# One trunk layer on one core: values of a head and output gates of its neighbour in one unit of 512 streamed columns

## The chip, the cores and the metric

The kernel runs on one core of one Trainium2 chip. The metric is the device time of one execution in microseconds (us); lower is better. All matrix products run in fp32r, each as three products of high and low parts (high x high, high x low, low x high), so that the result has nearly fp32's precision.

## The reference

One layer (DEPTH = 1): an mLSTM token mixer with a residual norm, then a top-2 mixture of 16 experts, then a gated embedding. The change lies in the mixer's input projection. Cut to that:

```python
# x: (1, 1024, 1024); A_HEADS = 4, A_DK = 128, A_DV = 256
def mlstm_mixer(x, w_in, conv_w, gate_b, norm_g, w_out):
    z = x @ w_in
    qk, v, o, gates = jnp.split(z, [2 * nqk, 2 * nqk + nv, 2 * nqk + 2 * nv], axis=-1)
    qk = silu(causal_depthwise_conv(qk, conv_w))
    ...
    h = mlstm_chunkwise(q, k, v, log_i, log_f)      # needs q, k, v of the head, and the gates
    y = head_rms_norm(h, norm_g) * sigmoid(o)       # o: output gates, 256 columns for each head
    return y @ w_out
```

## The kernel before

The 1024 tokens are eight tiles (t) of 128; the model width is eight blocks (k) of 128. `x` lies transposed in SBUF as high and low parts (XH, XL). The mixer works by units, each a slice of the input projection's columns:

- `qk_units` (u = 0 to 7: query and key of a head): the weights are the stationary operand, 512 tokens stream past them.
- `v_unit(h)` (256 columns of values; head 0 has the 8 gate columns besides): for each tile 24 products (eight k, three terms), with a block of x as the stationary operand and 256 columns of weights streaming. The result goes to VH, VL.
- `o_unit(h)` (256 columns of output gates): the same 24 products for each tile; ScalarE takes the sigmoid (`sg`), SyncE writes it to DRAM (`sig_d`).

`load_w` brings a raw piece of at most 1056 columns by SyncE's queue (`wr`, 3 buffers), ScalarE makes its high part (`wh`, 4 buffers), VectorE its low part (`wl`, 4 buffers). A unit of 256 columns has two pieces of four k each; a query or key unit has one.

`rec(h)` is the recurrence of a head over eight chunks: score, numerator (`nu`) and state update (`U`) on TensorE with small steps on ScalarE, VectorE and GpSimd between them; each chunk's numerator is written to DRAM (`num_d`). The code's order is

```python
        for h in range(H):
            rec(h)
            if h + 1 < H:
                v_unit(h + 1)
            if h + 2 < H:
                qk_units(2 * h + 4)
                qk_units(2 * h + 5)
            else:
                o_unit(h - 2, o_weights(h - 2))
        w2 = o_weights(2)
        pr.close()
```

so gates of heads 0 and 1 are traced within the loop, those of heads 2 and 3 behind it. The kernel is built with a list scheduler: it sets each engine's instruction order when the kernel is built, and mixes a recurrence with the unit that follows it; on the chip each engine runs its order as it stands.

`pr.close()` gives back the recurrence's memory. The output projection's weights take its room (`wout` pool; `load_wout`, L426): eight pieces through the same three `wr` buffers, ScalarE makes `woh` (scaled by the norm's gain `ng`), VectorE makes `wol`. `hs` (in the tile `spc`) is the heads' norm factor, from the denominators and sums of squares of all chunks of all heads. `mixed(t)` loads a tile's numerators (`nm`) and gates (`sgm`), multiplies them with `hs`, and splits them into `yh` (ScalarE) and `yl` (GpSimd for tile 0, VectorE for tile 1); TensorE transposes them (`tr`), ScalarE evicts (`yt`). `project` is the output projection of a tile: 24 products of 512 columns for each half of the model width, in the order of k, which read `woh` and `wol` of that k.

Of the kernel before, what the change touches and what calls it, by code (L numbers as in the profile page):

```python
# [13 lines left out]
F32 = mybir.dt.float32  # L14
# [10 lines left out]
D = 1024  # L25
NT = T // 128
ND = D // 128
H = 4
# [17 lines left out]
def trunk(ctx, tc, io, out):  # L46
# [77 lines left out]
    # ------------------------------------------------ token mixer  # L124
    pw = ExitStack()
    with ExitStack() as pa:
# [34 lines left out]
        def first_load():  # L161
            """the first units' weights and columns of x, in the order of their use"""
# [18 lines left out]
        def qk_units(*us, first=False, between=lambda: None):  # L181
            """the convolved queries or keys of heads; between is traced after half of the products"""
# [28 lines left out]
        def vo_weights(src, n):  # L211
            w = [load_w(src[:, 4 * i:4 * i + 4], 4 * n) for i in range(2)]
            return [[t.rearrange("p (k c) -> p k c", k=4) for t in p] for p in w]

        def vo_product(ps, w, t):
            half, o = divmod(t, 4)
            for k in range(ND):
                wh, wl = w[k // 4]
                xh = XH[half][:, k, 128 * o:128 * o + 128]
                xl = XL[half][:, k, 128 * o:128 * o + 128]  # L220
                product(ps, [(xh, wh[:, k % 4]), (xh, wl[:, k % 4]), (xl, wh[:, k % 4])],
                        k == 0, k == ND - 1)
# [3 lines left out]

        def v_unit(h):
            n = 264 if h == 0 else 256
            w = vo_weights(io["wv0"] if h == 0 else io["wv"][h - 1], n)
            for t in range(NT):  # L230
                ps = pmm.tile([128, 512], F32, name="mm")
                vo_product(ps[:, :n], w, t)
                vh = rp.tile([128, 258], F32R, name="vh", bufs=9)
# [8 lines left out]
        def o_weights(h):  # L242
            return vo_weights(io["wo"][h], 256)

        def o_unit(h, w):
            for t in range(NT):
                ps = pmm.tile([128, 512], F32, name="mm")
                vo_product(ps[:, :256], w, t)
                sg = wpool.tile([128, 256], F32, name="sg", bufs=2)
                S.activation(sg, ps[:, :256], AF.Sigmoid)  # L250
                SP.dma_start(sig_d[t, :, h], sg)
# [6 lines left out]
        def gates():  # L258
            """the gates' running sums and maxima, in two steps"""
# [125 lines left out]
        for h in range(H):  # L385
# [8 lines left out]
            if h + 2 < H:  # L394
                qk_units(2 * h + 4)
                qk_units(2 * h + 5)
            else:
                o_unit(h - 2, o_weights(h - 2))
        w2 = o_weights(2)
        pr.close()  # L400

        # output projection's weights and first rows, beside the last of the input projection
# [33 lines left out]
        o_unit(2, w2)  # L436
        for k in range(ND):
            if k == 2:
                w3 = o_weights(3)
            load_wout(k)  # L440

        def turned(src, q, hi, lo, n=128):
            """the parts of the transposes of four blocks of columns"""
# [5 lines left out]
        def transposed(p, hi, lo, tagbase):  # L449
            """the transposes of [128, D] parts, and the steps that make them"""  # L450
# [14 lines left out]
        def mixed(t, p):  # L465
            """a tile's gated heads and their parts, in steps; the last leaves the transposes"""
# [13 lines left out]
        o_unit(3, w3)  # L480
# [12 lines left out]
    # ------------------------------------------------ experts' parts  # L493
# [10 lines left out]
    def new_piece(kind):  # L504
        """kind: 0 and 1 for the first products' weights, 2 for the second's"""
# [7 lines left out]
    def queue_piece(raw, shape, kind, eng=None):  # L513
        """a piece whose split is queued, to be traced among the products"""
# [16 lines left out]
    def use(piece):  # L531
        """a piece's parts, after its split"""
# [4 lines left out]
    def splits(n):  # L537
        """the next n of the queued splits"""
# [3 lines left out]
    def tick():  # L542
        """after a step of products: every second a queued split, if the clock runs"""
# [6 lines left out]
    def load_part(fetch, m, eng=None, kind=None):  # L550
        """the two pieces of an expert's m-th weights"""
# [9 lines left out]
    def find_tokens(e, parts, nt=NT, p=None, pi=None):  # L561
        """tokens of slots: e [128 tokens, nt, slots] marks a slot's token; parts: ranges of slots"""
# [1152 lines left out]
```

## Time and profile before

| | |
|---|---|
| time, median of 3 runs | 1011.89 us (1011.25 to 1013.51) |
| span of the profiled execution | 1008.3 us |
| its own time: span and what lies around it | about 1011.9 us (3.6 us around the span, from the median) |
| TensorE busy | 973.3 us (97%), 5596 matmuls |
| VectorE, ScalarE, GpSimd busy | 667.0, 561.8, 302.0 us |
| mixer, up to the first transposes of the gated heads | 0 to 330.4 us |

A matmul's busy time overlaps its neighbours', so TensorE's pace is read from the distance of two starts and not from the mean duration. An instruction waits for the one ahead of it on its engine, also where that one waits for another engine or a DMA.

### The profile page before, as it was taken

What the parts mean: (1) busy time and instruction counts of PE and PEld (TensorE: products, weight loads), DVE (VectorE), ACT (ScalarE), POOL (GpSimd) and SP (SyncE); (2) the same over time, 40 slices, a digit from 0 to 9 for tenths busy, and PEclk for the clock granted to TensorE, in tenths of its full rate; (3) what the DMA queues carried; (4) which work ended last, traced back from release to release, by engine and by line L of the source; (5) the groups of instructions that cost most, each with busy time, mean ns of one, the idle gap of its engine ahead of it and who ended that gap; (6) DMA issues with size and microseconds to landing.
All of it is one profiled execution on the core that took longest, in us unless ns stands there. A gap on an engine that the chain in (4) does not pass through costs nothing. (4 is left out here: it accounts for less than half of the span.)

```text
span 1008.3 us, 15211 instructions
## 1 busy us (share of the span) xinstructions
PE 973.3 (97%) x5596; PEld 823.0 (82%) x5596; DVE 667.0 (66%) x1217; ACT 561.8 (56%) x928; POOL 302.0 (30%) x269
## 2 busy tenths in 40 slices
PE   7999999999999999997789999999999999989998
PEld 5989999899999887886467687878787878767887
DVE  6567667461542578879966689866657575577883
ACT  6346546363562455665447666766767676653431
POOL 0002203030100112225647424334252524354442
PEclk9999999999999999999979999999999999999999
DMA  8126811203354364522657998989898988754531
GB/s 320 47 69 266 305 58 59 84 33 93 101 183 155 136 251 150 187 67 117 223 177 289 377 330 290 342 290 335 297 336 298 342 325 296 268 194 149 184 127 63
DMA packets 51396, 207.05 MB, mean 205 GB/s; under 512 B 6892, under 2 KB 15724, under 8 KB 38264
## 3 DMA queue, kind: packets, MB, share of 16 engines
q1 hardware_dynamic: 43720, 182.74, 50.4%
q0 software_dynamic: 5824, 21.50, 6.1%
q10 hardware_dynamic: 1776, 1.81, 0.5%
q8 instruction: 45, 0.74, 0.3%
q14 instruction: 31, 0.25, 0.1%
HBM read 170.35 MB, written 35.68 MB: 204 GB/s over the span
## 5 line engine op out<-in xcount | busy, mean ns | idle before, releaser
L523 POOL TENSOR_TENSOR wlo<-wraw,whi 128x1024 fp32r<-128x1024 f32 x64 | 166.2, 2615 | 223.9 <-ACT whi L522 211.4
L522 ACT ACTIVATE whi<-wraw 128x1024 fp32r<-128x1024 f32 x204 | 205.5, 1051 | 12.9 <-DMA wraw<-eu 4.3
L523 DVE TENSOR_TENSOR wlo<-wraw,whi 128x1024 fp32r<-128x1024 f32 x140 | 172.5, 1259 | 38.8 <-ACT whi L522 37.7
L63 PE MATMUL mm<-whi,xt 128*128 128x512 f32 (+1 forms) x528 | 171.9, 396 | 2.2 <-DVE xt L58 1.5
L63 PE MATMUL mm<-wl,xh 128*128 128x256 f32 (+1 forms) x512 | 145.9, 285 | 0.0
L63 PE MATMUL mm<-wh,xh 128*128 128x256 f32 (+1 forms) x512 | 145.6, 284 | 0.0
L63 PE MATMUL mm<-wh,xl 128*128 128x256 f32 (+1 forms) x512 | 145.4, 284 | 0.0
L63 PEld LDWEIGHTS mm<-whi,xt 128*128 128x128 f32 x528 | 98.6, 191 | 23.7 <-DVE xt L58 2.0
L63 PE MATMUL mm<-wlo,xt 128*128 128x512 f32 (+1 forms) x264 | 100.9, 391 | 4.5 <-DVE wlo L523 4.5
L63 PEld LDWEIGHTS mm<-wh,xh 128*128 128x128 f32 x512 | 97.0, 189 | 0.1
L63 PEld LDWEIGHTS mm<-wl,xh 128*128 128x128 f32 x512 | 96.9, 189 | 0.1
L63 PEld LDWEIGHTS mm<-wh,xl 128*128 128x128 f32 x512 | 96.9, 189 | 0.0
L63 PE MATMUL mm<-woh,yt 128*128 128x512 f32 x256 | 93.6, 412 | 0.0
L63 PE MATMUL mm<-whi,ht 128*128 128x512 f32 x240 | 87.4, 413 | 2.3 <-ACT ht L57 1.4
L63 PE MATMUL mm<-whi,x2t 128*128 128x512 f32 (+1 forms) x272 | 84.7, 386 | 0.4 <-ACT x2t L57 0.4
L63 PEld LDWEIGHTS mm<-wlo,xt 128*128 128x128 f32 x264 | 49.5, 191 | 14.2 <-DVE wlo L523 4.9
L63 PEld LDWEIGHTS mm<-whi,x2t 128*128 128x128 f32 x272 | 50.1, 188 | 11.2 <-ACT x2t L57 0.9
L58 DVE TENSOR_TENSOR wl<-wr,wh 128x1024 fp32r<-128x1024 f32 (+2 forms) x26 | 29.7, 1144 | 44.3 <-ACT wh L57 44.0
L63 PE MATMUL mm<-xh,wh 128*128 128x512 f32 x128 | 50.7, 405 | 7.1 <-ACT xh L57 7.1
L63 PEld LDWEIGHTS mm<-whi,ht 128*128 128x128 f32 x240 | 45.5, 190 | 13.5 <-ACT ht L57 2.0
L63 PEld LDWEIGHTS mm<-woh,yt 128*128 128x128 f32 x256 | 48.1, 188 | 8.8
L63 PE MATMUL mm<-whi,xm 128*128 128x512 f32 x128 | 52.7, 412 | 0.0
(381 smaller groups left out, 2042.2 us busy)
## 6 DMA issues: line engine op xcount, KB each, us to landing
wraw<-eg SPq DMA_DIRECT2D x32, 1024.0 KB, 7.0
wraw<-ed SPq DMA_DIRECT2D x32, 1024.0 KB, 6.3
wraw<-eu SPq DMA_DIRECT2D x31, 1024.0 KB, 6.5
y_d<-zt SPq DMA_DIRECT2D x16, 512.0 KB, 5.6
y_d<-yo SPq DMA_DIRECT2D x14, 512.0 KB, 6.2
num_d<-nb SPq DMA_DIRECT2D x32, 128.0 KB, 1.8
wr<-wo SPq DMA_DIRECT2D x8, 512.0 KB, 4.6
sig_d<-sg SPq DMA_DIRECT2D x32, 128.0 KB, 1.8
```

The source lines that it names most:

```text
L58: (eng or V).tensor_tensor(lo, src, f32(hi), op=ALU.subtract)
L63: PE.matmul(ps, a, b, start=start and i == 0, stop=stop and i == n - 1)
L522: S.activation(hi[:, c], raw[:, c], AF.Copy)
L523: e.tensor_tensor(lo[:, c], raw[:, c], f32(hi)[:, c], op=ALU.subtract)
```

## The change

The output gates no longer have units of 256 columns. Values of head 1 and gates of head 0 share a unit of 512 columns, as do values of head 2 and gates of head 1; values of head 3 stay a unit of 256; gates of heads 2 and 3 are one unit of 512 behind the loop. A piece of weights still has 1024 columns, so a unit of 512 has four pieces of two k each. The unit with both gates has its weights asked for (`w2`) after the values of head 3, and there is nothing else behind `rec(3)` in the loop. The host's layout of the weights follows. (The change also drops comments and docstrings, which moves line numbers.)

```diff
-        def vo_weights(src, n):
-            w = [load_w(src[:, 4 * i:4 * i + 4], 4 * n) for i in range(2)]
-            return [[t.rearrange("p (k c) -> p k c", k=4) for t in p] for p in w]
-
-        def vo_product(ps, w, t):
+        def vo_weights(src):
+
+            n = src.shape[2]
+            m = 1056 // n
+            w = [load_w(src[:, m * i:m * i + m], m * n) for i in range(ND // m)]
+            return m, [[t.rearrange("p (k c) -> p k c", k=m) for t in p] for p in w]
+
+        def vo_product(ps, mw, t):
             half, o = divmod(t, 4)
+            m, w = mw
             for k in range(ND):
-                wh, wl = w[k // 4]
+                wh, wl = (a[:, k % m] for a in w[k // m])
...
+        def gate_rows(t, ps, *hs):
+
+            for i, h in enumerate(hs):
+                sg = wpool.tile([128, 256], F32, name="sg", bufs=2)
+                S.activation(sg, ps[:, 256 * i:256 * i + 256], AF.Sigmoid)
+                SP.dma_start(sig_d[t, :, h], sg)
+
         def v_unit(h):
-            n = 264 if h == 0 else 256
-            w = vo_weights(io["wv0"] if h == 0 else io["wv"][h - 1], n)
+
+            src = io["wv0"] if h == 0 else io["wvo"][h - 1] if h < H - 1 else io["wv3"]
+            n = src.shape[2]
+            w = vo_weights(src)
             for t in range(NT):
                 ps = pmm.tile([128, 512], F32, name="mm")
                 vo_product(ps[:, :n], w, t)
+                if n == 512:
+                    gate_rows(t, ps[:, 256:], h - 1)
...
-        def o_unit(h, w):
+        def o_unit(w):
+
             for t in range(NT):
                 ps = pmm.tile([128, 512], F32, name="mm")
-                vo_product(ps[:, :256], w, t)
-                sg = wpool.tile([128, 256], F32, name="sg", bufs=2)
-                S.activation(sg, ps[:, :256], AF.Sigmoid)
-                SP.dma_start(sig_d[t, :, h], sg)
+                vo_product(ps, w, t)
+                gate_rows(t, ps, H - 2, H - 1)
...
                 qk_units(2 * h + 5)
-            else:
-                o_unit(h - 2, o_weights(h - 2))
-        w2 = o_weights(2)
+            elif h + 1 < H:
+                w2 = vo_weights(io["woo"])
         pr.close()
...
-        o_unit(2, w2)
+        o_unit(w2)
         for k in range(ND):
-            if k == 2:
-                w3 = o_weights(3)
             load_wout(k)
...
-        o_unit(3, w3)
         yt, chain = list(mixed(0, yp))[1]
```

TensorE, the end of `rec(3)` before: the last of its numerators stands here among the products of the unit of head 1's gates (256 columns).

```order
L63 MATMUL mm<-wl,xh_118 128x256
L63 MATMUL nu<-CL,sh 128x258
L63 MATMUL nu<-CH,sl 128x258
L63 MATMUL nu<-vh,ph 128x258
L63 MATMUL nu<-vl,ph 128x258
L63 MATMUL nu<-vh,pl 128x258
L63 MATMUL mm<-wh,xl_120 128x256
```

Behind these rows stand 399 more products of 256 columns (the rest of that unit and the units of heads 2 and 3), and then the transposes of the first gated tile:

```order
L63 MATMUL mm<-wh,xl_120 128x256
L459 MATMUL tr<-identr,yh 128x128 x4
L459 MATMUL tr<-identr,yl 128x128 x4
L459 MATMUL tr<-identr,yh 128x128 x4
L459 MATMUL tr<-identr,yl 128x128 x4
L63 MATMUL mm<-woh_3982,yt_4276 128x512
```

TensorE, the same place with the change: `rec(3)` is spread over the eight tiles of the unit of both gates, and its last numerator stands in the last of them, behind two of that tile's 24 products.

```order
L63 MATMUL mm<-wh,xh_118 128x512
L63 MATMUL mm<-wl,xh_118 128x512
L63 MATMUL nu<-CL,sh 128x258
L63 MATMUL nu<-CH,sl 128x258
L63 MATMUL nu<-vh,ph 128x258
L63 MATMUL nu<-vl,ph 128x258
L63 MATMUL nu<-vh,pl 128x258
L63 MATMUL mm<-wh,xl_120 128x512
```

The tile's other 21 products follow, and then the same transposes, with two products of the output projection among them:

```order
L63 MATMUL mm<-wh,xl_120 128x512
L466 MATMUL tr<-identr,yh 128x128 x4
L63 MATMUL mm<-woh_3618,yt_3676 128x512
L63 MATMUL mm<-wol_3619,yt_3676 128x512
L812 MATMUL pi<-cs,ones 128x32
L466 MATMUL tr<-identr,yl 128x128 x4
L466 MATMUL tr<-identr,yh 128x128 x4
L466 MATMUL tr<-identr,yl 128x128 x4
L63 MATMUL mm<-woh_3618,yt_3677 128x512
```

So between the last numerator and the first transpose stood 400 products of 256 columns, and now stand 22 of 512.

ScalarE behind the last numerator's eviction (`nb`, `sq`), before: the eight `woh` stand among the gates' sigmoids (`sg`), and `yh` of tile 0 behind all of them.

```order
L351 ACTIVATE sq,spc<-nu 128x256
L57 ACTIVATE wh<-wr 128x1024
L250 ACTIVATE sg<-mm 128x256
L409 DMA ng<-ng 128x8
L412 DMA rr<-rw 128x128
L413 DMA lncol<-lncol 128x16
L421 ACT_TABLE_LOAD
L421 ACTIVATE tmp<-tmp,epsc 128x32
L250 ACT_TABLE_LOAD
L250 ACTIVATE sg<-mm 128x256
L431 ACTIVATE woh_3982<-wr,ng 128x1024
L431 ACTIVATE woh_3988<-wr,ng 128x1024
```

With the change, behind the same eviction and the three DMA issues and the square root, two sigmoids are left; three `woh` stand ahead of them and five among the evictions of the transposes (`yt`) that the output projection reads.

```order
L440 ACTIVATE woh_3630<-wr,ng 128x1024
L234 ACT_TABLE_LOAD
L234 ACTIVATE sg<-mm 128x256 x2
L798 DMA st_3730<-st 32x16
L57 ACTIVATE yh<-nm 128x1024
L57 ACTIVATE RW<-gr 128x8x16
L440 ACTIVATE woh_3636<-wr,ng 128x1024
L467 ACTIVATE yt_3676<-tr 128x512
L440 ACTIVATE woh_3642<-wr,ng 128x1024
L467 ACTIVATE yt_3677<-tr 128x512
L467 ACTIVATE yt_3676<-tr 128x512
L467 ACTIVATE yt_3677<-tr 128x512
```

Behind these rows stand `woh` of k = 5 and 6, `yh` of tile 1, and `woh` of k = 7. VectorE's order there is `wol` 0, `nm` of tile 0, the router's weights, `wol` 1 to 4, `nm` of tile 1, `wol` 5 and 6, `yl` of tile 1, `wol` 7. SyncE's is `nm`, `sgm` of tile 0, `wr` 3, the last tile's two gate writes, `sgm` of tile 1, `wr` 4 and 5, `nm` of tile 1, `wr` 6 and 7.

## Rows read from the trace of the kernel before

**Rows 1.** The head of the profile's page: the span, and the busy time of the engines (share of the span, instructions).

```profile
span 1008.3 us, 15211 instructions
PE 973.3 (97%) x5596; PEld 823.0 (82%) x5596; DVE 667.0 (66%) x1217; ACT 561.8 (56%) x928; POOL 302.0 (30%) x269
```

**Rows 2.** Busy time by window, for the mixer from the first pass of the recurrence on (84 to 307 us) and for the last output-gate unit (307 to 331 us): window, its length, then for each engine the busy microseconds and, in brackets, the instructions; then the granted TensorE clock (1.00 is 2.4 GHz), the DMA engines' busy share and GB/s.

```profile
84.00:307.00 223.00, 223.00 (x1699) 214.99 (x1698) 120.08 (x279) 118.19 (x306) 35.23 (x103) 1.00 0.38 129
307.00:331.00 24.00, 24.00 (x207) 24.00 (x206) 7.07 (x19) 5.89 (x13) 2.40 (x1) 1.00 0.39 125
```

**Rows 3.** Timeline of TensorE (start, duration, line, operation) in the last output-gate unit: the first and the last of its 192 products of 256 columns, 191 steps apart.

```profile
307.56 0.28 PE L63 MATMUL mm<-wh,xh 128*128 128x256 f32 x1
...
330.27 0.28 PE L63 MATMUL mm<-wh,xl 128*128 128x256 f32 x1
```

**Rows 4.** Timeline of TensorE in the query and key units of heads 2: 18 products of 512 columns right behind the recurrence's own products (17 steps), and 47 further on (46 steps).

```profile
125.00 0.40 PE L63 MATMUL mm<-xl,wh 128*128 128x512 f32 x1
...
128.95 0.39 PE L63 MATMUL mm<-xh,wh 128*128 128x512 f32 x1
129.18 0.39 PE L63 MATMUL mm<-xl,wh 128*128 128x512 f32 x1
...
139.60 0.39 PE L63 MATMUL mm<-xh,wl 128*128 128x512 f32 x1
```

**Rows 5.** Timeline of TensorE where the mixer ends: the recurrence's last product of the last head, the first transpose of tile 0's gated heads, and of the output projection's first 24 products (columns 0 to 511 of tile 0) the first and the last (the first of the two in its row).

```profile
282.72 0.28 PE L63 MATMUL nu<-vh,pl 128*128 128x258 f32 x1
...
330.39 0.46 PE L459 MATMUL tr<-identr,yh 128*128 128x128 f32 x4
...
332.06 0.46 PE L63 MATMUL mm<-woh,yt 128*128 128x512 f32 x1
...
337.72 0.63 PE L63 MATMUL mm<-woh,yt 128*128 128x512 f32 x2
```

**Rows 6.** Timeline of ScalarE (ACT; ACTq is its queue of DMA issues) from the recurrence's last eviction on.

```profile
283.04 0.38 ACT L348 ACTIVATE nb<-nu 128x256 f32<-128x256 f32 x1 [1.28 <-PE nu L63]
...
283.59 0.20 ACT L351 ACTIVATION_READ_ACCUMULATOR sq<-nu 128x1 f32 x1
...
284.94 0.39 ACT L250 ACTIVATE sg<-mm 128x256 f32<-128x256 f32 x1 [0.20 <-PE mm L63]
...
286.28 1.28 ACT L421 ACT_TABLE_LOAD   x1 [0.96 <-issue]
287.58 0.32 ACT L421 ACTIVATE tmp<-tmp,epsc 128x32 f32<-128x32 f32 x1
...
289.49 2.18 ACT L431 ACTIVATE woh<-wr,ng 128x1024 fp32r<-128x1024 f32 x2
...
309.56 0.64 ACT L250 ACTIVATE sg<-mm 128x256 f32<-128x256 f32 x2
...
319.36 1.06 ACT L57 ACTIVATE yh<-nm 128x1024 fp32r<-128x1024 f32 x1 [2.60 <-DVE nm L472]
...
331.04 1.09 ACT L460 ACTIVATE yt<-tr 128x512 fp32r<-128x512 f32 x2
332.01 0.31 ACT L57 ACTIVATE RW<-gr 128x128 fp32r<-128x128 f32 x1
```

**Rows 7.** Timeline of VectorE (DVE): a low part of the output projection's weights, tile 0's gated heads (four instructions in one row), and the router's weights (two).

```profile
309.74 1.28 DVE L432 SCALAR_TENSOR_TENSOR wol<-wr,ng,woh 128x1024 fp32r<-128x1024 f32 x1 [1.50 <-ACT woh L431]
317.65 1.67 DVE L472 SCALAR_TENSOR_TENSOR nm<-nm,spc,sgm 128x256 f32<-128x256 f32 x4 [6.63 <-DMA sgm<-sig_d]
...
328.30 0.42 DVE L800 TENSOR_TENSOR gr<-rr,lncol 128x128 f32<-128x128 f32 x2
```

**Rows 8.** Timeline of GpSimd (POOL): the low part of tile 0's gated heads.

```profile
320.50 2.40 POOL L58 TENSOR_TENSOR yl<-nm,yh 128x1024 fp32r<-128x1024 f32 x1 [44.07 <-ACT yh L57]
```

**Rows 9.** DMA issues between 225 and 345 us: target<-source, queue, count, KB of one, median us from issue to landing.

```profile
nm<-num_d SPq DMA_DIRECT2D x3, 512.0 KB, 7.2
sgm<-sig_d SPq DMA_DIRECT2D x3, 512.0 KB, 3.6
...
ng<-ng ACTq DMA_DIRECT2D x1, 4.0 KB, 3.8
```

**Rows 10.** The tile `wr`, raw pieces of weights, between 225 and 345 us: its DMA issues, and the time from issue to landing.

```profile
L428 SPq DMA_DIRECT2D wr<-wout x8: 328/333/1428, 236.2 to 302.6; - x8
...
DMA to landing us min/median/max: 3.6/5.0/5.9
```

**Rows 11.** Busy time by window (columns as in rows 2) around 490 to 510 us.

```profile
490.80:494.20 3.40, 3.40 (x7) 1.99 (x7) 3.32 (x3) 1.87 (x4) 3.05 (x2) 0.50 1.00 410
501.50:506.20 4.70, 0.38 (x2) 0.00 (x0) 4.70 (x7) 0.84 (x1) 2.91 (x2) 0.81 0.31 124
506.20:510.00 3.80, 2.10 (x4) 1.40 (x5) 3.80 (x10) 2.17 (x3) 0.00 (x0) 0.50 0.29 41
```

**Rows 12.** Timeline of TensorE inside the first of those windows.

```profile
493.08 0.63 PE L63 MATMUL mm<-whi,xm 128*128 128x512 f32 x1
493.51 0.63 PE L63 MATMUL mm<-wlo,xm 128*128 128x512 f32 x1
```

**Rows 13.** What VectorE waited for between 345 and 470 us, the longest sum: us in total, times, longest.

```profile
DVE zres L843 <- PE mm L63: 8.9, 10, 2.1
```

More of the change, by code (lines that the diff above doesn't have):

```diff
@@ L209, in qk_units @@
                 QK[u] = a
-        def vo_weights(src, n):
-            w = [load_w(src[:, 4 * i:4 * i + 4], 4 * n) for i in range(2)]
-            return [[t.rearrange("p (k c) -> p k c", k=4) for t in p] for p in w]
-        def vo_product(ps, w, t):
+        def vo_weights(src):
[4 more added lines that the diff above has]
+        def vo_product(ps, mw, t):
             half, o = divmod(t, 4)
+            m, w = mw
             for k in range(ND):
-                wh, wl = w[k // 4]
+                wh, wl = (a[:, k % m] for a in w[k // m])
                 xh = XH[half][:, k, 128 * o:128 * o + 128]
                 xl = XL[half][:, k, 128 * o:128 * o + 128]
-                product(ps, [(xh, wh[:, k % 4]), (xh, wl[:, k % 4]), (xl, wh[:, k % 4])],
-                        k == 0, k == ND - 1)
+                product(ps, [(xh, wh), (xh, wl), (xl, wh)], k == 0, k == ND - 1)
         VH, VL = {}, {}
         zg = rp.tile([128, NT, 2 * H], F32, name="zg", bufs=1)
+        def gate_rows(t, ps, *hs):
[3 more added lines that the diff above has]
+                SP.dma_start(sig_d[t, :, h], sg)
         def v_unit(h):
-            n = 264 if h == 0 else 256
-            w = vo_weights(io["wv0"] if h == 0 else io["wv"][h - 1], n)
+            src = io["wv0"] if h == 0 else io["wvo"][h - 1] if h < H - 1 else io["wv3"]
+            n = src.shape[2]
+            w = vo_weights(src)
             for t in range(NT):
@@ L240, in v_unit @@
                 VH[h, t], VL[h, t] = vh, vl
-        def o_weights(h):
-            return vo_weights(io["wo"][h], 256)
-        def o_unit(h, w):
+        def o_unit(w):
             for t in range(NT):
                 ps = pmm.tile([128, 512], F32, name="mm")
-                vo_product(ps[:, :256], w, t)
-                sg = wpool.tile([128, 256], F32, name="sg", bufs=2)
-                S.activation(sg, ps[:, :256], AF.Sigmoid)
-                SP.dma_start(sig_d[t, :, h], sg)
+                vo_product(ps, w, t)
+                gate_rows(t, ps, H - 2, H - 1)
         g4 = lambda name: rp.tile([128, NT, H], F32, name=name, bufs=1)
@@ L1671, in _layout @@
     d["wv0"] = kp(np.concatenate([w[:, v0:v0 + DV], w[:, g0:]], axis=1))
-    d["wv"] = np.stack([kp(w[:, v0 + h * DV:v0 + h * DV + DV]) for h in range(1, H)])
-    d["wo"] = np.stack([kp(w[:, o0 + h * DV:o0 + h * DV + DV]) for h in range(H)])
+    wv, wo = ([w[:, c + h * DV:c + h * DV + DV] for h in range(H)] for c in (v0, o0))
+    d["wvo"] = np.stack([kp(np.concatenate([wv[h], wo[h - 1]], axis=1)) for h in range(1, H - 1)])
+    d["wv3"] = kp(wv[H - 1])
+    d["woo"] = kp(np.concatenate(wo[H - 2:], axis=1))
     cv = c(mlstm_conv)[0].T.reshape(2, H, 128, 4)
```

## Prediction

> **What bounds the kernel now.** I read the page's head first: TensorE is busy 97% of 1008.3 us [rows 1]. A busy share says little about pace, so the windows come next. From 84 to 331 us TensorE has no idle time at all, while VectorE works 120 of 223 us in the first stretch and only 7.1 of 24 in the second, ScalarE 118 and 5.9 [rows 2]. The mixer is bound by how fast TensorE takes its columns, and its last 24 us leave the other engines nearly free. The timeline then gives the pace. 256 columns: 191 steps from 307.56 to 330.27 us, 118.9 ns each [rows 3]. 512 columns: 17 steps beside the recurrence in 3.95 us, 232.4 ns, and 46 quiet steps in 10.42 us, 226.5 ns [rows 4]. Both run at the full clock. Last I read the end of the mixer on each engine [rows 5 to 8], since the change moves what stands there.
>
> **What the streams gain.** Before, seven units (three of values, four of gates) have 8 x 24 products of 256 columns, 1344 in all. Now three units have 192 of 512 columns and one has 192 of 256. So 1152 products of 256 become 576 of 512. A pair of the old took 2 x 118.9 = 237.8 ns [rows 3]. The trace has no 512-column product with these operands; the nearest rows bound it between 226.5 and 232.4 ns [rows 4]. In all three units a recurrence runs beside for most of the time, so I weight the row beside it twice: 230.5 ns. The gain is 576 x 7.3 ns = 4.2 us, between 3.1 (232.4) and 6.5 (226.5). The Trainium skill, "TensorE: Matmul & The Clock Gate", section "Back-to-back issue gap", gives columns over 2.4 GHz and 2.5 ns for a product alone: 109.2 and 215.8 ns. The rows are 8 to 9% above at 256 columns and 5 to 8% at 512; by the page a pair would save 2.5 ns, and the gain would be an estimated 1.5 us instead of 4.2.
>
> **What costs nothing.** Pieces of weights stay fourteen, each with the same split; sigmoids stay 32 of 256 columns, now two waits on a tile fewer. A unit of 512 takes all four `wh` and `wl` buffers, so the next unit's pieces are split only while its last tile runs. The first piece is free with 18 products left, 4.1 us; a split takes 1.06 us on ScalarE and 1.23 on VectorE (the second piece's shape, [rows 6, 7], is the same 1024 columns at 1.1 and 1.3 us). That is hidden. Without the cover each unit's start would cost some 2.4 us, four times. The recurrence's small steps have more time than before: a chunk falls on a tile of 24 x 230.5 ns = 5.5 us.
>
> **The hole behind the mixer.** Before, rec(3) issues its last numerator at 282.72 us and the first transpose of tile 0 comes at 330.39 [rows 5]: 47.7 us of gate products, in which ScalarE and VectorE prepare the eight pieces of output weights, `hs`, and tile 0. With the change 22 products of 512 stand there, 5.1 us. The preparation reads chunk 8's sums and takes the recurrence's memory, so in the new order it still starts behind the last numerator. I count from the issue of that numerator and take each step from the rows:
> - ScalarE's evictions end at 1.1 (283.79 - 282.72) [rows 6]. The gain `ng` is asked for then and lands 3.8 us later [rows 9]: 4.9. Three DMA issues, the table load of 1.28 us and the root fit ahead of that.
> - `woh` 0 to 2 at 1.09 us [rows 6]: 8.2. Table load for the sigmoid 1.28, two sigmoids 0.64, a DMA issue 0.4: 10.5. `yh` 1.06: 11.6. RW 0.3: 11.9 [rows 6].
> - VectorE meanwhile: `wol` 0 until 7.3 (1.28), `nm` 1.67 until 9.0, router 0.42, `wol` 1 until 10.6, `wol` 2 until 11.8 [rows 7].
> - Raw piece 3 can be asked for when `wol` 0 has freed its buffer, 7.4; pieces land in 5.0 us, 3.6 to 5.9 [rows 10]: 12.4. `woh` 3 until 13.6, and behind it the first `yt` (0.6) until 14.1.
> - Piece 4 waits on SyncE behind the last tile's gate writes, and for `wol` 1: asked at 10.7, lands at 15.7, `woh` 4 until 16.9. Three `yt` stand behind it: 18.5. Only then has TensorE the low part of tile 0.
> - Piece 5 has landed by 16.9, `woh` 5 until 19.7. Then `nm` of tile 1, whose load waits for `yl` of tile 0 on GpSimd (11.6 + 2.4 = 14.0) [rows 8] and lands 3.6 to 7.2 us later [rows 9], 17.8 to 21.3. `wol` 5 and 6 queue behind it on VectorE; `woh` 7 waits on ScalarE behind `yh` of tile 1, which needs it too. Piece 7 lands at 23.2. `wol` 7 ends between 25.7 and 28.1.
> - The first 24 projection products end 0.5 us behind `wol` 7: 26.2 to 28.6.
>
> Without a wait they would end at 12.8: the tile's 5.1 and 0.1 ahead of it, and 7.6 us for transposes and 24 products, as between 330.39 and 337.95 now (337.72 and one step) [rows 5]. The hole is 13.4 to 15.8 us. If all pieces and `nm` lay ready, ScalarE's own row of work remains (11.9, then five `woh`, four `yt`, `yh`: 21.0, with `wol` 7 and two products 22.7), and the hole is 9.9. I take 14.0, in the lower half of the row-by-row count, as single pieces land in 3.6 us; 9.9 and 15.8 are the ends.
>
> **The clock in the hole.** TensorE idles about 6 us there and then works in pieces. The rows show what followed such idleness: between 501.5 and 506.2 us it was busy 0.38 of 4.7 us, and the next 3.8 us were granted 0.50; so was the stretch from 490.8 [rows 11], where products stand 0.43 us apart [rows 12] instead of 0.23. A stretch of 3.4 us at 1.2 GHz holds 7.9 products instead of 14.8 and loses 1.6 us if TensorE has work. I take one such stretch, +1.6; nothing if it falls into the waiting, 3.2 if two meet work. The same page of the Trainium skill, section "HAM oscillation", says of bursts between waits that each restart is cold; this trace agrees at 490.8 and 506.2 us.
>
> **Sum.** -4.2 + 14.0 + 1.6 = +11.4 us: a span of 1019.7 us. About 3.6 us lie around the span in the median run (1011.9 - 1008.3), so the time is 1023.3 us.
>
> **Rivals.**
> - The pieces land early and the clock holds: the hole is ScalarE's 9.9 us, 1011.9 - 4.2 + 9.9 = 1017.6. For it: the shortest landing is 3.6 us, and nothing else loads then. Against: piece 4's request waits for `wol` 1, not for bandwidth.
> - The other side: the stage behind takes the hole in. VectorE is the other busy engine there; if it were late anyway, TensorE's delay would vanish in its waits, and the time would be 1011.9 - 4.2 = 1007.7. It decides for faster once 11.4 of the 15.6 us are taken in. Against: VectorE's longest wait between 345 and 470 us is for TensorE's products, 8.9 us in ten waits [rows 13], so it follows TensorE and a late product makes it late.
> - A larger hole: pieces at 5.9 us, `nm` at 7.2, two cold stretches, 3.1 us of gain: 1011.9 - 3.1 + 16 + 3.2 = 1028.
> - The change doesn't do what it says, and 512 columns cost two of 256: 1027.5, inside the range.
>
> **How the numbers follow.** The row-by-row case (1020 to 1026.5) has 0.6, early pieces 0.2, the larger hole and the vain change together 0.12, taken in 0.06, and 0.02 for a partly hidden hole within 0.2% (2 us, about what a measurement tells from no change). 1023.3 is the first case. The range 1015.5 to 1028 takes in the first three at their bounds. Faster 0.05, same 0.03, slower 0.92.
>
> **What would show it.** Right: steps of 226 to 233 ns in the three wide units, no TensorE idle time ahead of rec(3)'s last numerator, this numerator some 5 us ahead of the last gate product, then a hole in which TensorE waits for `yh`, `yt`, `woh` and `wol`, and a granted clock of 0.5 in or behind it; everything behind shifted by the hole less the gain. Wrong: idle time at the starts of the wide units (splits late), steps under 220 ns (a larger gain), or a first projection half that ends within 16 us of the last numerator.

## The result, and the profile with the change

The changed kernel takes 1020.89 us (median; 1016.63 to 1021.73), the kernel before 1011.57 in the same comparison: a ratio of 1.008 (over all runs, not from the two medians), 95% interval 1.0057 to 1.0102. Forecast were 1023.3 us, 1015.5 to 1028, and slower with a chance of 0.92. The profiled execution spans 1019.9 us, 11.6 more than the one before; the sum had said +11.4.

The head of the page with the change:

```profile
span 1019.9 us, 14061 instructions
PE 975.0 (96%) x5020; PEld 798.8 (78%) x5020; DVE 670.0 (66%) x1217; ACT 566.1 (56%) x932; POOL 304.2 (30%) x269
```

TensorE has 576 matmuls fewer than in [rows 1], as counted. A busy share that falls from 97 to 96% says little of where 11.6 us went. First the pace, from TensorE's timeline: the first wide product and the one behind it, the first and the last of 18 wide products inside the unit of both gates, the last numerator of `rec(3)`, and the unit's last product.

```profile
85.77 0.47 PE L63 MATMUL mm<-wh,xh 128*128 128x512 f32 x1
86.08 0.39 PE L63 MATMUL mm<-wl,xh 128*128 128x512 f32 x1
...
299.83 0.39 PE L63 MATMUL mm<-wl,xh 128*128 128x512 f32 x1
...
303.74 0.40 PE L63 MATMUL mm<-wh,xh 128*128 128x512 f32 x1
...
322.62 0.29 PE L63 MATMUL nu<-vh,pl 128*128 128x258 f32 x1
...
327.57 0.39 PE L63 MATMUL mm<-wh,xl 128*128 128x512 f32 x1
```

17 steps from 299.83 to 303.74 are 230.0 ns each (230.5 was taken). None of the recurrence's products stands in that stretch; a wide product right behind one of them can take longer, as the first one does (310 ns, 85.77 to 86.08). From the first wide product to the unit's last one it is 241.80 us. Before, the same stretch began here and ended at the last row of [rows 3]:

```profile
84.58 0.36 PE L63 MATMUL mm<-wh,xh 128*128 128x256 f32 x1
```

330.27 - 84.58 = 245.69, so the mixer's streams gained 3.9 us. Behind them, TensorE's timeline with the change:

```profile
332.00 0.54 PE L466 MATMUL tr<-identr,yh 128*128 128x128 f32 x4 [4.05 <-ACT yh L57]
333.73 0.80 PE L63 MATMUL mm<-woh,yt 128*128 128x512 f32 x1 [1.18 <-ACT yt L467]
...
336.30 0.64 PE L812 MATMUL pi<-cs,ones 128*128 128x32 f32 x2 [1.35 <-DVE cs L810]
...
343.75 0.50 PE L63 MATMUL mm<-wol,yt 128*128 128x512 f32 x1 [1.01 <-DVE wol L441]
...
347.28 0.51 PE L63 MATMUL mm<-wol,yt 128*128 128x512 f32 x1 [0.96 <-DVE wol L441]
347.62 0.63 PE L63 MATMUL mm<-woh,yt 128*128 128x512 f32 x2
```

The second product of the last row, at 347.85, is the 25th of the projection: 20.28 us behind the unit's last product, where it was 7.69 before (337.96 - 330.27, [rows 3, 5]). The hole is 12.6 us. The chain of work that ended last in this stretch (start, duration, what) says who made it:

```profile
324.26 4.81 DMA sgm<-sig_d
...
329.59 1.27 DVE nm L479 x3
...
332.38 3.39 DVE wol L441
...
335.78 0.33 SPq L437
...
336.21 4.49 DMA nm<-num_d
...
342.42 1.09 DVE wol L441
...
343.61 1.02 DVE wol L441
...
344.81 1.12 DVE yl L58
...
345.94 1.29 DVE wol L441
```

ScalarE's timeline in the same stretch has the gain's request, the first three high parts and `yh`, VectorE's the first `nm`, GpSimd's `yl`:

```profile
322.95 0.33 ACTq L418 DMA_DIRECT2D ng<-ng  x1
...
325.81 3.21 ACT L440 ACTIVATE woh<-wr,ng 128x1024 fp32r<-128x1024 f32 x3
...
330.89 1.06 ACT L57 ACTIVATE yh<-nm 128x1024 fp32r<-128x1024 f32 x1
```

```profile
329.19 1.67 DVE L479 SCALAR_TENSOR_TENSOR nm<-nm,spc,sgm 128x256 f32<-128x256 f32 x4 [0.93 <-DMA sgm<-sig_d]
```

```profile
332.03 2.65 POOL L58 TENSOR_TENSOR yl<-nm,yh 128x1024 fp32r<-128x1024 f32 x1 [19.95 <-ACT yh L57]
```

In the chain, the load of tile 1's numerators is asked for only at 336.21, since it stands on SyncE behind the raw piece of 335.78, which waits until `wol` has freed its buffer; and `wol` 5 to 7 stand behind tile 1's product on VectorE. The clock, by window (columns as in [rows 2]):

```profile
332.00:334.60 2.60, 1.42 (x6) 0.90 (x6) 2.60 (x2) 1.67 (x3) 2.57 (x1) 0.73 0.90 230
334.60:340.00 5.40, 3.99 (x19) 3.17 (x19) 4.56 (x7) 3.11 (x5) 0.07 (x1) 0.50 0.87 301
340.00:347.90 7.90, 5.56 (x21) 3.40 (x20) 6.40 (x8) 3.89 (x4) 0.00 (x0) 1.00 1.00 360
```

After 4.1 us of standing TensorE worked in pieces and was granted 0.50, 1.2 GHz, until 340 us. Once it ran at full clock it had to wait again for `wol` (1.01 and 0.96 us in the rows above).

The rest of the 11.6 us: the 25th projection product to the first expert product took 120.7 us before and 122.9 now (+2.2); from there to the end 549.6 and 549.1 (-0.5); and the first wide product came 1.2 us later (85.77 for 84.58), although nothing ahead of it was changed. In sum 1.2 - 3.9 + 12.6 + 2.2 - 0.5 = 11.6.

### The profile page after: what moved, and what is told of

Its sections match the earlier page's. It is cut to its first block, busy times and chain, and to the rows that moved or that the text cites. A ratio compares the mean times of both kernels' runs of the same rounds, so it can differ in the third digit from the quotient of the medians.

```text
span 1019.9 us, 14061 instructions
## 1 busy us (share of the span) xinstructions
PE 975.0 (96%) x5020; PEld 798.8 (78%) x5020; DVE 670.0 (66%) x1217; ACT 566.1 (56%) x932; POOL 304.2 (30%) x269
## 4 chain that ended last, share of the span: by engine, by line
PE 81%; DVE 10%; DMA 4%; ACT 2%; issue 2%; POOL 1%; SPq 0%; DVEq 0%; ACTq 0%; POOLq 0%
PE mm L63 71%; PE tr L453 3%; PE nu L63 2%; DVE wlo L529 1%; ACT whi L528 1%; PE tr L466 1%; DVE shift L865 1%; DVE nm L479 1%; PE U L63 1%; DMA wraw<-eu 1%; POOL wlo L529 1%; DVE wol L441 1%; PE sm L343 1%; DVE zres L873 1%; DMA wr<-wqk 1%
## 5 line engine op out<-in xcount | busy, mean ns | idle before, releaser
L63 PE MATMUL mm<-wl,xh 128*128 128x512 f32 (+2 forms) x320 | 112.9, 353 | 0.0
L63 PE MATMUL mm<-wh,xl 128*128 128x512 f32 (+2 forms) x320 | 112.7, 352 | 0.0
L63 PE MATMUL mm<-wh,xh 128*128 128x512 f32 (+2 forms) x320 | 112.1, 351 | 0.0
L63 PEld LDWEIGHTS mm<-wh,xh 128*128 128x128 f32 x320 | 60.3, 189 | 7.1
L63 PEld LDWEIGHTS mm<-wl,xh 128*128 128x128 f32 x320 | 60.4, 189 | 7.1
L63 PEld LDWEIGHTS mm<-wh,xl 128*128 128x128 f32 x320 | 60.3, 188 | 7.0
L63 PE MATMUL mm<-wol,yt 128*128 128x512 f32 x128 | 51.4, 401 | 2.2 <-DVE wol L441 2.2
## 6 DMA issues: line engine op xcount, KB each, us to landing
y_d<-yo SPq DMA_DIRECT2D x14, 512.0 KB, 11.6
```

What stands on the lines that cost most here:

```text
L63: PE.matmul(ps, a, b, start=start and i == 0, stop=stop and i == n - 1)
```

## The experiments

The table takes its first four columns from the traces: pairs of 256 columns that became one of 512; the mixer from the first product beside `rec(0)` to the last product of the last unit; the cover from the last numerator of `rec(3)` to that product; the hole, which is the time from that product to the 25th of the projection, less the 7.69 us of before. These agree to 0.1 us between kernels that share the code in question. The time is the median, and the ratio is to the kernel before on the same chip, over all runs and with its 95% interval. The change keeps the ratio of its own comparison (1011.57 before); the 1009.7 of the first row belongs to the others (1009.7 to 1009.8).

| kernel | pairs | mixer | cover | hole | time, ratio |
|---|---|---|---|---|---|
| before | 0 | 245.69 | 47.6 | 0 | 1009.7 |
| change | 576 | 241.80 | 5.0 | 12.6 | 1020.9, 1.008 (1.0057 to 1.0102) |
| bcov | 0 | 245.64 | 3.4 | 17.9 | 1030.2, 1.0204 (1.018 to 1.0228) |
| nall | 0 | 245.25 | 24.5 | 2.8 | 1008.5, 0.9989 (0.9969 to 1.0008) |
| n8 | 384 | 243.00 | 24.5 | 2.9 | 1006.6, 0.9973 (0.9955 to 0.9992) |
| w1t | 384 | 242.93 | 46.7 | 0.0 | 1008.1, 0.9998 (0.998 to 1.0015) |
| n4 | 480 | 242.31 | 23.8 | 3.4 | 1009.3, 0.9986 (0.9965 to 1.0007) |
| n4erw | 480 | 242.31 | 23.8 | 0.0 | 1008.1, 0.9999 (0.9975 to 1.0022) |
| n2 | 528 | 241.99 | 15.6 | 5.3 | 1012.6, 1.0028 (1.0011 to 1.0044) |
| n2erw3 | 528 | 241.99 | 15.6 | 1.2 | 1010.3, 1.0003 (0.9986 to 1.002) |
| n1 | 552 | 241.90 | 8.4 | 12.0 | 1019.1, 1.0087 (1.0055 to 1.0119) |
| ylv | 576 | 241.80 | 5.0 | 12.7 | 1021.5 (one time) |
| erw | 576 | 241.80 | 5.0 | 16.1 | 1018.6, 1.0094 (1.0065 to 1.0124) |
| erw3 | 576 | 241.80 | 5.0 | 8.6 | 1013.8, 1.0041 (1.0016 to 1.0065) |

**Narrow tiles in the unit of both gates (n1, n2, n4, n8).** A number of its tiles (four in n4, shown here; one, two and eight in n1, n2 and n8) are computed as two products of 256 columns. The recurrence's chunks go into the order tile by tile, so narrower tiles bring its last numerator forward, and wide ones stand behind it.

```diff
-        def vo_product(ps, mw, t):
+        def vo_product(ps, mw, t, c=slice(0, None)):
...
-                wh, wl = (a[:, k % m] for a in w[k // m])
+                wh, wl = (a[:, k % m, c] for a in w[k // m])
...
             for t in range(NT):
+                for i in range(2 if t < 4 else 0):
+                    ps = pmm.tile([128, 512], F32, name="mm")
+                    vo_product(ps[:, :256], w, t, slice(256 * i, 256 * i + 256))
+                    gate_rows(t, ps, H - 2 + i)
+                if t < 4:
+                    continue
                 ps = pmm.tile([128, 512], F32, name="mm")
                 vo_product(ps, w, t)
                 gate_rows(t, ps, H - 2, H - 1)
```

> The changed kernel, but tiles 0 to 3 of the unit of both gates are computed as two products of 256 columns instead of one of 512 (same weights, same order of units). In the built order rec(3) then ends in the middle of that unit, and 96 products of 512 and 15 of 256 stand behind its last numerator: 23.9 us of cover instead of 5.1. Cover theory: the changed kernel's first projection half ended 25.2 us behind the last numerator, 7.6 of which is its own work, so 17.6 us of cover are needed; here there is no hole, and 480 pairs of 256 columns saved at 7.3 ns each give 3.5 us: about 1008.1 us. Rival, wide products gain nothing: 1011.6. Rival, the loss comes from the wide units themselves (weights in four pieces, later pieces) and not from the end of the mixer: 1018 to 1020 as before this edit.

> The changed kernel with all eight tiles of the unit of both gates as pairs of 256 columns; values of heads 1 and 2 keep their wide units. 207 products of 256 columns stand behind the last numerator, 24.6 us. Cover theory: no hole, 384 pairs saved, 2.8 us: 1008.8 us. Wide products gain nothing: 1011.6. Loss from the wide units themselves: above 1015.

Measured: the mixer shrank by 3.4 and 2.7 us, as expected to 0.1 (nall, below, shows that 0.4 of each is not the width's), and the hole from 12.6 to 3.4 and 2.9 us, not to nothing. The streams' gain and the greater part of the hole are thus two things that can be had apart. Where the 3.4 us of n4 come from, ScalarE's timeline and then TensorE's and the clock's:

```profile
327.57 1.15 ACT L446 ACTIVATE woh<-wr,ng 128x1024 fp32r<-128x1024 f32 x1 [3.14 <-DMA wr<-wout]
...
329.15 1.57 ACT L473 ACTIVATE yt<-tr 128x512 fp32r<-128x512 f32 x3
```

```profile
329.80 0.55 PE L472 MATMUL tr<-identr,yl 128*128 128x128 f32 x4 [1.16 <-ACT yt L473]
```

```profile
331.40:334.90 3.50, 3.50 (x10) 2.83 (x11) 1.66 (x4) 0.95 (x3) 0.00 (x0) 0.52 0.93 356
```

The last high part waits 3.14 us for its raw piece, the evictions stand behind it, TensorE stands for 1.16 us (and 0.40 for the column sums), and then runs 3.5 us at half clock, products 0.43 us apart. The standing is 1.6 us. The eight products from 331.53 to 335.04 us took 3.5 us; eight at the 0.23 us of full clock take 1.9, so the clock cost 1.6.

> The changed kernel with only tile 0 of the unit of both gates as pairs of 256 columns: 37 products of 512 stand behind the last numerator, 8.5 us of cover. Cover theory with 17.6 us needed: a hole of 9.1 us, 552 pairs saved. The gate clock's cold stretch in or behind it. If the hole hangs on something else than the cover, it stays at 12.6 (changed kernel) or vanishes.

> Tiles 0 and 1 as pairs of 256: 68 products of 512 behind the last numerator, 15.7 us of cover. Cover theory with 17.6 us needed: a hole of 1.9 us, up to 5 if the yt stand behind late high parts on ScalarE as in the run with four narrow tiles (3.4 at 23.9 us of cover). 528 pairs saved, 3.9 us.

Measured: 12.0 and 5.3 us, for 9.1 and 1.9 (up to 5). The hole falls with the cover, but not one for one: from the last numerator to the 25th projection product it takes 25.2 us with the change, 28.1 in n1, 28.6 in n2, 34.9 in n4. The preparation has no length of its own. It gets longer where more gate tiles follow it: their sigmoids and writes stand in the same queues, and the order changes. What each of the two costs was not separated. In n1 VectorE's `nm` of tile 0 stands ahead of `wol` 0, and TensorE waits for the column sums (`cs`) that come behind them. The router's weights `gr` ahead of the sums also took longer: 2.58 us for two, where two took 0.48 with the change, beside GpSimd's `yl`, which ran from 329.99 to 332.51.

```profile
325.95 1.28 DVE L485 SCALAR_TENSOR_TENSOR nm<-nm,spc,sgm 128x256 f32<-128x256 f32 x3 [2.94 <-DMA sgm<-sig_d]
327.14 1.28 DVE L447 SCALAR_TENSOR_TENSOR wol<-wr,ng,woh 128x1024 fp32r<-128x1024 f32 x1
...
330.07 2.58 DVE L812 TENSOR_TENSOR gr<-rr,lncol 128x128 f32<-128x128 f32 x2
```

```profile
334.60 0.63 PE L818 MATMUL pi<-cs,ones 128*128 128x32 f32 x2 [2.68 <-DVE cs L816]
```

**No wide product at all (nall).** As n8, and the two wide units with values are also computed as pairs of 256.

```diff
-                vo_product(ps[:, :n], w, t)
+                m = min(n, 264)
+                vo_product(ps[:, :m] if n < 512 else ps[:, :256], w, t, slice(0, m if n < 512 else 256))
                 if n == 512:
-                    gate_rows(t, ps[:, 256:], h - 1)
+                    p2 = pmm.tile([128, 512], F32, name="mm")
+                    vo_product(p2[:, :256], w, t, slice(256, 512))
+                    gate_rows(t, p2, h - 1)
```

> The changed kernel's units and weights, but no product of 512 columns in them: every tile of the three wide units is two products of 256 columns. 24.6 us of cover. If the gain is that of wide products alone, nothing is gained and nothing lost: 1011.6 us, and the step between products of 256 columns is 118.9 ns. If the new order of the units gains or costs by itself, this run shows it: the gain seen in the other two runs would be here too (1008 to 1009).

Measured: a mixer of 245.25 us, 0.4 under that of before. So the units' new order and four-piece weights are worth 0.4 together, and the products' width the rest: 2.25 us for 384 pairs (n8), 2.94 for 480, 3.26 for 528, 3.45 for 576, which is 5.9 to 6.2 ns a pair in these kernels. (w1t, below, has another order and no such twin.)

**The kernel before without its cover (bcov).** Units of 256 columns with two pieces each, but the gates of heads 0 to 2 ahead of `rec(3)`, and those of head 3 behind it.

```diff
                 v_unit(h + 1)
+            if h in (1, 2):
+                o_unit(h - 1, o_weights(h - 1))
...
-            else:
-                o_unit(h - 2, o_weights(h - 2))
-        w2 = o_weights(2)
+            elif h == 2:
+                o_unit(2, o_weights(2))
+                w3 = o_weights(3)
         pr.close()
...
-        o_unit(2, w2)
+        o_unit(3, w3)
```

> The kernel before (all units of 256 columns, weights in two pieces), but with the gates of heads 0 to 2 ahead of rec(3), so that only 29 products of 256 columns, 3.4 us, stand behind its last numerator. Cover theory: a hole of 17.6 - 3.4 = 14.2 us without any wide product: 1025.8 us. Rival, the hole is made by the wide unit (four pieces, more columns per tile, later sigmoids): 1011.6.

Measured: a hole of 17.9 us, and 1030.2 us. There is no wide product in it, so the hole comes from what stands behind the last numerator, not from the units' width. It is 3.7 us longer than expected; TensorE's first wait alone is 8.24 us:

```profile
330.53 0.28 PE L63 MATMUL mm<-wh,xl 128*128 128x256 f32 x1
339.06 0.75 PE L459 MATMUL tr<-identr,yh 128*128 128x128 f32 x4 [8.24 <-ACT yh L57]
```

ScalarE could not make `yh` earlier, since VectorE's product for it (`nm`) waited for the gates' load and was then cut in two by `wol` 0:

```profile
335.04 0.48 DVE L472 SCALAR_TENSOR_TENSOR nm<-nm,spc,sgm 128x256 f32<-128x256 f32 x1 [3.44 <-DMA sgm<-sig_d]
335.44 1.28 DVE L434 SCALAR_TENSOR_TENSOR wol<-wr,ng,woh 128x1024 fp32r<-128x1024 f32 x1
336.64 1.27 DVE L472 SCALAR_TENSOR_TENSOR nm<-nm,spc,sgm 128x256 f32<-128x256 f32 x3
```

It began 7.95 us behind the last numerator (330.53 - 3.44 = 327.09) and ended at 10.8; with the change it began at 6.6 and ended at 8.2. So 1.4 of these 2.6 us are the gates' load, which came later, and 1.2 are `wol` 0 in the midst of the product. So a lack of cover is enough for a hole; what another order would take off its length was not tried here.

**One wide gate unit behind rec(3), all of it cover (w1t).** Values of head 2 and gates of head 1 are units of 256 again; gates of head 1 run beside `rec(3)`.

```diff
-            src = io["wv0"] if h == 0 else io["wvo"][h - 1] if h < H - 1 else io["wv3"]
+            src = io["wv0"] if h == 0 else io["wvo"][h - 1] if h == 1 else io["wvo"][1][:, :, :256] if h == 2 else io["wv3"]
...
+        def o_one(w):
+            for t in range(NT):
+                ps = pmm.tile([128, 512], F32, name="mm")
+                vo_product(ps[:, :256], w, t)
+                gate_rows(t, ps, 1)
...
-            elif h + 1 < H:
+            elif h + 1 == H:
+                o_one(vo_weights(io["wvo"][1][:, :, 256:]))
                 w2 = vo_weights(io["woo"])
```

> Only values of head 1 with gates of head 0 and the two last heads' gates are wide; values of head 2 and gates of head 1 are units of 256 columns again, and gates of head 1 run beside rec(3), so that 192 products of 512 and 21 of 256 stand behind its last numerator: 46.8 us of cover, as before the change (47.6). Cover theory: no hole, 384 pairs saved, 2.8 us: 1007.0. If the unit of both gates costs by itself (four pieces, both sigmoids of a tile together): 1010 or more.

Measured: the mixer 2.8 us shorter, no hole. TensorE's timeline, last product, transposes and projection without a wait:

```profile
327.56 0.39 PE L63 MATMUL mm<-wh,xl 128*128 128x512 f32 x1
327.79 0.46 PE L473 MATMUL tr<-identr,yh 128*128 128x128 f32 x4
...
335.05 0.63 PE L63 MATMUL mm<-woh,yt 128*128 128x512 f32 x2
```

The 25th projection product is the second of the last row, 7.72 us behind the first. Yet the time, 1008.1, cannot be told from that of before (1009.8). In the profiled runs the projection's remaining stretch took 122.8 us here and 120.7 before; there TensorE waited, between 348 and 470 us (us in total, times, longest; first w1t, then before; two more waits, 1.2 us for `xt` and 0.7 for `whi`, are the same in both):

```profile
PE pi L896 <- DVE lt L894: 3.4, 3, 1.4
PE tr L473 <- ACT mv L867: 1.7, 1, 1.7
```

```profile
PE pi L883 <- DVE lt L881: 2.4, 3, 1.4
...
PE tr L459 <- DVE xl L58: 0.6, 1, 0.6
```

With those two it is 7.0 us for 4.9: 1.0 more on the router's logits (`lt`), and a first wait of 1.7 us behind a row's norm factor (`mv`, with a table load of 1.28 us ahead of it on ScalarE) in place of 0.6 for a row's low part (`xl`). The difference of 2.1 us is about what the stretch grew, so in this execution most of the gain was given back there. Its span was still 2.8 us shorter than that of before, as the code behind the first expert product, which is the same in both, took 2.1 us less; the last section has more on such differences.

**Raw pieces early (erw, n4erw).** Pieces 3 to 7 land in the room of the first half of x, which is free after tile 3 of the unit.

```diff
-            raw = wpool.tile([128, 1056], F32, name="wr", tag="wr", bufs=3)[:, :D]
+            if k < 3:
+                raw = wpool.tile([128, 1056], F32, name="wr", tag="wr", bufs=3)[:, :D]
+            else:
+                raw = XR[(k - 3) // 4][:, k - 3 if k < 7 else 0]
...
         o_unit(w2)
+        XR = [xpool.tile([128, 4, D], F32, name=n, tag=n) for n in ("xl0", "xh0")]
```

> The changed kernel with one edit: raw pieces 3 to 7 of the output weights go into the room of the first half of x (free once tile 3 of the unit of both gates is done) instead of the three shared buffers, so all eight lie ready before rec(3) ends. In the built order all eight high parts then stand ahead of yh of tile 0 on ScalarE. Theory that the pieces' route (buffers, landing, SyncE) sets the hole: it shrinks from 12.5 us to ScalarE's own row of work, about 10; the granted clock still falls. Rival, the route costs nothing beside ScalarE's row: it stays at 12.5. Rival, the route is nearly all: under 6. Read from the trace as the time from the unit's last product to the start of the 25th projection product, less 7.7.

Measured: the hole grew to 16.1 us. With the pieces there, the order that was built puts all eight high parts ahead of `yh` on ScalarE, and TensorE waits for it:

```profile
334.72 1.04 ACT L57 ACTIVATE yh<-nm 128x1024 fp32r<-128x1024 f32 x1
```

```profile
335.82 0.75 PE L470 MATMUL tr<-identr,yh 128*128 128x128 f32 x4 [9.21 <-ACT yh L57]
```

None of the three outcomes was met: the pieces' wait was gone, and ScalarE's row had a worse order.

> The run with tiles 0 to 3 narrow had 23.9 us of cover and still lost 3.4 us behind the mixer: yt waited on ScalarE behind the last high part, whose raw piece came late, TensorE stood for 1.3 and 0.6 us, and a cold stretch followed. With the raw pieces early as well that wait should go: no hole, and the 3.5 us of the 480 saved pairs remain. Mean of the kernel before in the first call 1009.8: 1006.3 expected. If the rest of the hole has another cause (the column sums that TensorE waits for, the router's weights), it stays near 1009.

Measured: no hole (0.03 us), so late pieces were what n4 had left. But the time is 1008.1, not 1006.3, and the same as that of before within its interval.

**The early pieces with an order by hand (erw3, n2erw3).** ScalarE and VectorE keep the order in which this is written:

```diff
-        for k in range(ND):
+        for k in range(3):
             load_wout(k)
...
-        yt, chain = list(mixed(0, yp))[1]
-        for _ in chain:
-            pass
+        with tc.manual_schedule(engines={mybir.EngineType.Activation, mybir.EngineType.DVE}):
+            yt, chain = list(mixed(0, yp))[1]
+            for k in (3, 4):
+                load_wout(k)
+            for i, _ in enumerate(chain):
+                if i in (0, 3):
+                    load_wout(5 + i // 3)
+            load_wout(7)
```

> The early raw pieces again (3 to 7 in the room of the first half of x), but ScalarE's and VectorE's order behind the first three high parts written out by hand: yh of tile 0 right behind the last two sigmoids, then two high parts, and the other three between and behind the four yt. With the early pieces alone yh stood behind all eight high parts and the hole grew from 12.6 to 16.1 us. If landing and buffers and ScalarE's order set the hole together, it falls here to what ScalarE's row of work leaves, 8 to 10 us (9.9 in the prediction). If the pieces' route never mattered, it is 12.6 again.

Measured: 8.6 us, within the 8 to 10 expected, and 1013.8 us. Buffers and order together take 4.0 us out of the hole with the cover unchanged. TensorE's waits are now the two that rest on the recurrence's end:

```profile
331.49 0.53 PE L470 MATMUL tr<-identr,yh 128*128 128x128 f32 x4 [4.10 <-ACT yh L57]
335.01 0.75 PE L470 MATMUL tr<-identr,yl 128*128 128x128 f32 x4 [2.99 <-POOL yl L58]
```

> Tiles 0 and 1 as pairs of 256 (15.7 us of cover), early raw pieces, and the order of ScalarE and VectorE by hand. With the preparation shortened to about 14 us behind the last numerator the cover holds: no hole (7.7 us from the unit's last product to the 25th projection product), 528 pairs saved, 3.9 us less in the mixer, and a time of 1006 to 1008 against 1009.5 for the kernel before. If 3 us or more are lost behind the mixer again, the preparation needs more than 15.7 us even so: 1009 or more.

Measured: a hole of 1.2 us instead of none, and 1010.3 us: no difference from before can be told. Its stretch behind the first projection half was the longest but one of all (124.1 us for 120.7).

**The low part of tile 0 on VectorE (ylv).**

```diff
-            split(yh, yl, nm.rearrange("p h e -> p (h e)"), V if t == 1 else G)
+            split(yh, yl, nm.rearrange("p h e -> p (h e)"), V if t < 2 else G)
```

> The changed kernel with the low part of tile 0's gated heads on VectorE instead of GpSimd. In the changed kernel the third low part of the output weights took 3.38 us instead of 1.28 while GpSimd worked on that low part. If the two engines hinder each other, the third low part takes 1.28 us here, the low part itself about 1.22 on VectorE, and the raw piece that waits for its buffer is asked for earlier; the hole shrinks by 1 to 2 us, from 12.5 to about 11. If the 3.38 us were a wait for something else (its raw piece), it stays.

Measured: `wol` by tile (minimum, median, maximum in ns), first with the change, then here:

```profile
L441 DVE SCALAR_TENSOR_TENSOR wol<-wr,ng,woh x8: 1275/1278/3375, 327.0 to 345.9; 128x1024 fp32r<-128x1024 f32 x8
```

```profile
L441 DVE SCALAR_TENSOR_TENSOR wol<-wr,ng,woh x8: 1280/1280/1286, 326.4 to 345.5; 128x1024 fp32r<-128x1024 f32 x8
```

The third `wol` took 1.28 us instead of 3.38, so the two engines had hindered each other. The hole did not shrink to 11 as expected: 12.7 us. Tile 1's numerators were asked for 12.65 instead of 13.6 us behind the last numerator, but ScalarE's eighth high part then waited 1.39 us for its raw piece.

## Why the prediction was right, and what was off

- **Streams.** The step of 230.5 ns was right where nothing stands between the products (230.0). The gain was 3.9 us for 4.2, of which 3.45 by the width: 6.0 ns a pair, not 7.3; the other 0.4, from order and pieces, was not forecast and brought the sum nearer by luck. The pair's 237.8 ns had been read in a unit without a recurrence beside it; why a pair beside one saves less was not taken apart. The rule of the Trainium skill ("TensorE: Matmul & The Clock Gate", section "Back-to-back issue gap"), which is for a product alone, gives an estimated 2.5 ns a pair; no run here agrees with that (5.9 to 6.2 ns).
- **What costs nothing.** Right: no idle time of TensorE at the wide units' starts; the mixer is the same to 0.01 us in four kernels, and the four-piece weights cost nothing (nall).
- **The hole.** Its place and cause were right: bcov has it without a wide product, w1t and n4erw have wide products without it. Its size was 12.6 for 14.0, below the count's own 13.4 to 15.8. The step that failed is the gain `ng`: it was counted as asked for behind ScalarE's evictions and as landed at 4.9 us. But its issue stood on ScalarE's own queue at 322.95, 0.3 us behind the numerator and not 1.1, and the first high part began without a wait behind the square root, at 3.2 us, so the gain had landed within 2.9 us and not 3.8. ScalarE's row came some 2 us earlier (`yh` ended at 9.3 for 11.6). Some of this was lost again: `wol` 2 took 3.4 us, and tile 1's `nm` was late by SyncE's queue (behind piece 5), not by GpSimd's `yl` as the prediction had it; the count's time for it, 14.0, was near the 13.6 measured for the wrong reason. The chain above does not pass through `ng`, so how much of the 1.4 us between 14.0 and 12.6 it made is not shown. The 25th product was forecast 26.2 to 28.6 us behind the numerator and came at 25.2.
- **The clock.** Right that it falls to 0.50, and n4 shows the priced case: a stretch of 3.5 us that costs 1.6, as priced. In the changed kernel itself it fell into the waiting, and the +1.6 of the sum was not paid; that was named as its lower bound.
- **The sum** met the span (+11.4 for +11.6) by luck, by errors that cancel: 3.0 us too much for hole and clock, against 0.3 too much gain and 2.9 us elsewhere that were not forecast (+1.2 at the start, +2.2 and -0.5 behind). The 3.6 us around the span were wrong too: the later runs show 2.3 for the kernel before and 1.8 for the change, so the median run of before had a longer span than the profiled one.
- **Rivals.** "The pieces land early", 9.9 us: with the pieces early the hole was 16.1, and 8.6 once ScalarE's order was mended, so the rival was near on what is left and wrong that landing alone decides it. "The stage behind takes the hole in": not seen. With no hole the rest of the projection took 120.7 (before), 122.7 and 122.8 us, with 12.6 us of hole 122.9, with 16.1 us 120.0. "512 columns cost two of 256": ruled out by the 3.45 us between nall and the change.

What stays open: the stretch behind the first projection half varies between 120.0 and 124.5 us over these kernels, partly with the waits for the router's logits, and I did not find a rule for it; and none of the versions without a hole could be shown to beat the kernel before by more than its spread. Only n8 was faster with an interval that leaves out 1 (0.9973), and that by traces is 2.7 us of gain with 2.9 of hole, so I don't take the time for a proof that this arrangement is better than n4erw's.

## What to carry to other kernels

Merging streams saves columns' overhead, but ask what the removed or merged pieces had been covering: here a gain of 3.9 us cost 12.6, as work that only the recurrence's end releases lost its cover. With an order that is fixed when the kernel is built, the granularity of the work beside a chain of dependent steps sets how far the chain is spread: a chunk went to each tile, so wider tiles put the chain's end against the unit's end. Count the release from the last link of that chain, on each queue, and look for what stands behind what; giving one wait away (early pieces) can worsen the order of the rest.

## What the runs showed of the hardware that was not expected

- VectorE and GpSimd exclude each other in turns. With the change `yl` ran on GpSimd from 332.03 to 334.68; a `wol` that began at 332.38 ended at 335.77, 1.09 us behind it, instead of after 1.28. In erw the wait fell on GpSimd, while VectorE ran its low parts at their usual pace:

```profile
332.33 4.87 DVE L444 SCALAR_TENSOR_TENSOR wol<-xl,ng,woh 128x1024 fp32r<-128x1024 f32 x4
```

```profile
335.85 4.74 POOL L58 TENSOR_TENSOR yl<-nm,yh 128x1024 fp32r<-128x1024 f32 x1 [25.12 <-ACT yh L57]
```

  The Trainium skill, "SBUF — State Buffer", section "SBUF: two separate sides", says that the two share a pair of ports that one instruction holds to its end; this trace agrees (4.74 and 3.38 us for 2.40 [rows 8] and 1.28).
- The same code takes different times in different executions. At the start of the program products stood 0.43 us apart until 12.5 us in the kernel before and until 15.7 with the change, and the first product beside `rec(0)` came between 84.42 and 85.82 us over these kernels, although nothing ahead of it differs. More lies at the other end: from the first expert product on, where all the kernels have the same instructions in the same order, the profiled executions took from 543.6 us (n2) to 550.5 (n4). The spans of the kernel before spread over some 8 us (1003.6 to 1012.3 in 29 runs), so that a gain of 3 us can be read from a trace's stretch to 0.1 us and hardly from the times.
